# Seven groups of a hybrid encoder block: nine pairs by seven products instead of eight, and four low parts a group made by adding transfers

## The chip, the core and the metric

The kernel runs on one core of one Trainium2 chip. The metric is the device time of one execution in microseconds; lower is better. Five engines matter: PE (TensorE, the matmuls; PEld is its weight load), DVE (VectorE), ACT (ScalarE), POOL (GpSimd) and SP (SyncE, which here only issues DMAs).

## What is computed

One layer of a hybrid streaming encoder, for 256 rows of 4096 float32 values. Cut to what matters:

```python
xn = rms_norm(h, norm_in_g)
proj = xn @ w_in                                  # 4096 x 14336
q, k, v, z_a, a_c, g_c, z_c = split(proj)
y_a = rms_norm(chunked_attention(q, k, v, rel_table), attn_out_g) * silu(z_a)
y_c = rms_norm(conv_module(a_c, g_c, ...), conv_out_g) * silu(z_c)   # one 2048 x 2048 product
h = h + concatenate([y_a, y_c], -1) @ w_out       # 4096 x 4096
gate = sigmoid(rms_norm(h, ple_norm_g) @ w_ple_gate + b_ple_gate)    # 4096 x 4096
h = h + gate * (p @ w_ple)
return rms_norm(h, final_g)
```

Nearly all the work is products of 256 rows with large weights that are read once from HBM.

## The kernel before

**Two parts of every number.** Each operand is split into a high part (a cast to fp32r, which TensorE reads in one pass) and a low part, the float32 value minus the high part, again as fp32r. A product of two blocks is three matmuls: high by high, low by high, high by low (`kind` 0, 1, 2). The weights are split on the fly: SP loads a weight tile `wt` (128 x 2 x 512 values, 512 KB), ScalarE casts it to `wh` (L204), VectorE subtracts to get `wl` (L205). There are five buffers for `wt`, three each for `wh` and `wl`, two each for `uh` and `ul` (below).

**Groups and pairs.** `mixed_product` computes one group: two column blocks of 512 by all 256 rows, accumulated in four PSUM banks over 32 blocks of 128 rows of weights, taken as 16 pairs. A plain pair is 2 blocks x 2 column blocks x 2 halves of the rows x 3 kinds = 24 matmuls. A pair "by sevens" replaces eight block products by seven, in the manner of Strassen and Winograd: P1 to P7, 21 matmuls. For that VectorE forms sums of weight blocks, `ua` (L469, L470) and `ub` (L476, L477), ScalarE and VectorE split them into `uh` and `ul`, and four sums of the left operand (`comb`, kept for each such pair) must have been made before. P1, P5, P6 and P7 collect in four more banks, which VectorE combines after the last pair by sevens (`on_helpers`, `helper_sums`) in two scratch tiles `z` from the pool's tag "stage", which has two buffers.

**The order of the pairs** is written out by hand in texts such as

```python
dense = units("1 0* 3 2* 5 4* 6* 7 8* 9 10* 11 12* 14* 13 15")
```

where a star marks a pair by sevens. A plus marks one whose `ua` is built by a load and a second, adding transfer from GpSimd (L422, L423); the attention and convolution groups use those. Every engine's queue is in order. The program's scheduler decides where instructions of different tiles stand on a queue.

**Stages, in order of time.** Convolution and attention groups of w_in (to about 920 us), two groups of w_pw, the combinations of xT for the coming groups, four groups of gates (`gated`, from about 987 us, order `dense`), four groups of the last projection w_out (the first with order `late`, from about 1316 us, then three with `dense`), four groups of w_ple_gate (to the end). Each gates group ends with products of z and the accumulators on VectorE, the activation Silu on ScalarE, and a last product that is put off (`later`) into the first pairs of the next group. The combinations for pairs by sevens with even numbers are made by `combine_again` and `combined_parts`.

Of the kernel before, what the change touches and what calls it, by code (L numbers as in the profile page):

```python
# [10 lines left out]
F32 = mybir.dt.float32  # L11
F32R = mybir.dt.float32r
# [13 lines left out]
def hybrid_block(  # L26
# [172 lines left out]
    def parts_of(wt, kc, tiles=None):  # L199
# [10 lines left out]
        return (wh, wl), made  # L210

    recent = []

# [46 lines left out]

    def combined_parts(dst, at, s, a, a01, a11, g, then=lambda ins: None):

        a00, a10 = a[:, :P], a[:, P:]
        s3, s5, s2, s4 = (s[:, i * P : (i + 1) * P] for i in range(4))
        stt = nc.vector.scalar_tensor_tensor
        then(nc.vector.tensor_tensor(s3, a00, a10, ALU.subtract))
        then(stt(s5, a11, g, a10, ALU.mult, ALU.subtract))
        then(stt(s2, s5, -1.0, a00, ALU.mult, ALU.subtract))  # L270
        then(stt(s4, a01, g, s2, ALU.mult, ALU.add))

        def split():
            hi, lo = dst[:, at : at + 2, 0, :], dst[:, at : at + 2, 1, :]
            src = s.rearrange("q (i t) -> q i t", t=T)
            then(nc.scalar.copy(hi, src))
            then(nc.vector.tensor_tensor(lo, src, hi.bitcast(F32), ALU.subtract))

        return split
# [6 lines left out]

    def combine_again(dst, at, t, i, rows, then=lambda ins: None):

# [6 lines left out]
        )  # L295
        return combined_parts(dst, at, s, a[:, :T], a[:, T : T + P], a[:, T + P :], 1.0, then)

# [26 lines left out]
    def units(text):  # L324

        return [(int(u.rstrip("*+")), u[-1] if u[-1] in "*+" else "") for u in text.split()]


    dense = units("1 0* 3 2* 5 4* 6* 7 8* 9 10* 11 12* 14* 13 15")
    first = units("0 1 3 5 7 9 11 13 15 2* 8 4* 10 6* 12 14")  # L330
    early = units("1 3 5 0+ 7 9 2+ 11 13 4+ 15 8 6+ 10 12 14")
# [9 lines left out]
    final = units("1 0* 3 2* 5 4* 6* 7 8* 9 10* 12* 11 13 14 15")  # L341
    late = units("1 3 5 7 9 11 13 15 0* 2 4* 6 8* 10* 12 14")

    def mixed_product(
# [13 lines left out]
        n_left = len(left) // 2  # L358
        for n, (_, seven) in enumerate(order[: len(order) - n_left]):
            for name in ("P1", "P5", "P6", "P7", "P2", "P3", "P4") if seven else ("P2", "P3", "P4", "X"):  # L360
                ends[name] = n
# [37 lines left out]
        def add_plain(n, k, wh, wl, **kw):  # L399
            pair = order[n][0]  # L400
            for j in range(2):
                for h in range(NH):
                    name = (("P2", "P3"), ("P4", "X"))[h][j]
                    add(name, block(2 * pair + k, h), (wh[:, j], wl[:, j]), n, k == 1, **kw)

        sums = {}

# [18 lines left out]
        if begin:  # L426
            done, behind = begin(add_plain)
            for ins in behind:
                after.enter_context(tc.issue_after(ins.ins))
        last_seven = max((n for n, (_, seven) in enumerate(order) if seven), default=None)  # L430
        for n, (pair, seven) in enumerate(order):
            if n < done:
# [18 lines left out]
            if not seven:  # L451
                for k in range(2):
                    add_plain(n, k, *parts_of(wts[k], 2)[0])
                fill(fills[n % len(fills)])
                continue
# [15 lines left out]
            with queued_behind(before if seven == "+" else ()):  # L471
                uah, ual = pair_parts(ua)
            w1h, w1l = parts_of(w1, 2)[0]
            if seven == "*" and not sums:
# [5 lines left out]

            def s_of(i):
                t, at = comb[pair] if isinstance(comb, dict) else (comb[pair // 4], pair % 4)
                return [t[:, at + i // 2, q, (i % 2) * P : (i % 2 + 1) * P] for q in range(2)]
# [4 lines left out]
            add("P7", s_of(0), (uah[:, 1], ual[:, 1]), n, True)  # L488
            add("P2", block(k1, 0), (w1h[:, 0], w1l[:, 0]), n, True)
            add("P3", s_of(3), (w1h[:, 1], w1l[:, 1]), n, True)  # L490
            add("P6", s_of(2), (ubh[:, 0], ubl[:, 0]), n, True)
            add("P4", block(k1, 1), (ubh[:, 1], ubl[:, 1]), n, True)
            if begins and on_begin:
                on_begin()
# [564 lines left out]
    for c in range(2, D // NB):  # L1059
        if c % 2 == 0:  # L1060
            comb_tile(xS, 1)
        combine_again(xS[c // 2], 2 * (c % 2), xT[c], 0, sum_rows())()

    def gated(ys, c0, col, r_y, order, ahead):

        _, z = sum_tiles()

        def on_helpers(helper):
            nc.scalar.copy(z[0][0], helper["P1"])
            helper_sums(helper, z)  # L1070
# [33 lines left out]
    for ys, o_z, r_y in ((y_a, o_za, r_a), (y_c, o_zc, r_c)):  # L1104
        for c0 in range(0, len(ys), 2):
            last = ys is y_c and c0 + 2 == len(ys)
            gated(
                ys, c0, o_z, r_y, dense,
                before_last(y_ahead) if last else None,
# [24 lines left out]
    for c0 in range(0, D // NB, 2):  # L1134
# [8 lines left out]
        def on_helpers(helper):  # L1143
# [8 lines left out]
        acc = mixed_product(  # L1152
            w_out[0], c0 * NB, yT, yS, dense if c0 else late, on_helpers,
            ahead=y_ahead if c0 == 0 else before_last(h_ahead) if c0 + 2 == D // NB else None,
            fills=(2,),
        )
        for h, j in QUARTERS:
            hc = hs[c0 + j][:, h, :]
            tt(hc, acc[h][j], hc, ALU.add)
            later.append(partial(square_sum, ssq_h[:, h, c0 + j : c0 + j + 1], hc))  # L1160
    fill(len(later))
    r_h = rstd_of(ssq_h, D, "r_h")
# [8 lines left out]
    def gated_pair(c0, order, ahead):  # L1171

        _, z = sum_tiles()
        rows, fgs = [], []

        def on_begin():
            rows.extend(broadcast_row(b_ple_gate, (c0 + j) * NB, NB) for j in range(2))

        def on_helpers(helper):
            stt(z[0][0], helper["P1"], r_h[:, :1], rows[0], ALU.mult, ALU.add)  # L1180
            helper_sums(helper, z)
# [178 lines left out]
```

## Time and profile before

| | us |
|---|---|
| three runs, median | 2028.87 |
| lowest and highest | 2028.55 and 2030.01 |
| the profiled execution: its span, first to last instruction | 2027.3 |

The median lies 1.6 us above the span of the profiled execution; the part outside the span is what a run needs ahead of the first and behind the last instruction. Of the profile the following views are used: the page (span, chain, costliest groups), the busy time by stretch, the waits, the timeline, and the DMA issues with their time to landing. In a row of groups stand the line, engine, operation, tiles (out<-in), the number of instructions, then busy us and mean ns of one, then idle time ahead of them and what ended it. In a row of waits stand who waited for whom, the us in total, the times, and the longest.

### The profile page before, as it was taken

What the parts mean: (1) busy time and instruction counts of PE and PEld (TensorE: products, weight loads), DVE (VectorE), ACT (ScalarE), POOL (GpSimd) and SP (SyncE); (2) the same over time, 40 slices, a digit from 0 to 9 for tenths busy, and PEclk for the clock granted to TensorE, in tenths of its full rate; (3) what the DMA queues carried; (4) which work ended last, traced back from release to release, by engine and by line L of the source; (5) the groups of instructions that cost most, each with busy time, mean ns of one, the idle gap of its engine ahead of it and who ended that gap; (6) DMA issues with size and microseconds to landing.
All of it is one profiled execution on the core that took longest, in us unless ns stands there. A gap on an engine that the chain in (4) does not pass through costs nothing.

```text
span 2027.3 us, 26222 instructions
## 1 busy us (share of the span) xinstructions
PE 2010.3 (99%) x9064; PEld 1652.2 (81%) x9064; DVE 1917.8 (95%) x2732; ACT 1222.7 (60%) x1591; POOL 46.9 (2%) x50
## 2 busy tenths in 40 slices
PE   9999999999999999999999999999999999999997
PEld 7888888878888888788888888888888888888876
DVE  7999999889999998888899999999999999999998
ACT  7655545665656556776556566676665666665555
POOL 0000000000000000000000000000000000000000
PEclk9999999999999999999999999999999999999999
DMA  8787878678669867556666666676666656666765
GB/s 293 222 237 236 253 219 249 177 227 256 192 198 268 251 202 239 157 176 213 192 210 204 206 203 214 210 239 209 203 210 199 208 191 204 207 219 205 233 206 181
DMA packets 171168, 436.70 MB, mean 215 GB/s; under 512 B 13966, under 2 KB 17182, under 8 KB 171034
## 3 DMA queue, kind: packets, MB, share of 16 engines
q1 hardware_dynamic: 161952, 417.93, 64.1%
q0 software_dynamic: 8432, 16.25, 4.7%
q8 instruction: 71, 1.16, 0.3%
q10 hardware_dynamic: 650, 0.84, 0.1%
q14 instruction: 63, 0.52, 0.1%
HBM read 430.77 MB, written 4.19 MB: 215 GB/s over the span
## 4 chain that ended last, share of the span: by engine, by line
PE 92%; DVE 4%; issue 2%; DMA 1%; ACT 1%; POOLq 0%; POOL 0%; ACTq 0%; DVEq 0%
PE acc L387 71%; PE acc_P L387 17%; DVE wl L205 1%; PE tmp_ps L170 1%; DVE cv L726 1%; PE acc L229 1%; DMA wt<-in_w_in_dram 1%; DVE ul L205 1%; PE tmp_ps L898 0%; PE tmp_ps L882 0%; PE tmp_ps L916 0%; DVE cv L807 0%; PE tmp_ps L921 0%; ACT uh L204 0%; PE acc L375 0%
## 5 line engine op out<-in xcount | busy, mean ns | idle before, releaser
L387 PE MATMUL acc<-wh,big_t 128*128 128x512 f32 x4112 | 1271.6, 391 | 0.9 <-DVE y_c L1051 0.7
L204 ACT CAST wh<-wt 128x1024 fp32r<-128x1024 f32 (+1 forms) x737 | 708.8, 972 | 514.6 <-PE acc L387 359.8
L387 PEld LDWEIGHTS acc<-wh,big_t 128*128 128x128 f32 x4112 | 768.9, 188 | 160.4 <-DVE y_c L1051 1.1
L205 DVE TENSOR_TENSOR wl<-wt,wh 128x1024 fp32r<-128x1024 f32 (+1 forms) x737 | 816.7, 1120 | 33.4 <-ACT wh L204 27.8
L387 PE MATMUL acc<-wl,big_t 128*128 128x512 f32 x2056 | 794.5, 392 | 0.1
L387 PEld LDWEIGHTS acc<-wl,big_t 128*128 128x128 f32 x2056 | 385.5, 188 | 81.6 <-DVE wl L205 2.0
L204 ACT CAST uh<-ua 128x1024 fp32r<-128x1024 f32 x180 | 189.4, 1052 | 95.9 <-DVE ua L470 46.4
L205 DVE TENSOR_TENSOR ul<-ua,uh 128x1024 fp32r<-128x1024 f32 x180 | 219.5, 1220 | 5.0 <-ACT uh L204 3.2
L726 DVE SCALAR_TENSOR_TENSOR cv<-uT,dw,cv 128x255 f32<-128x255 f32 (+23 forms) x480 | 204.2, 465 | 1.1
L387 PE MATMUL acc_P<-uh,big_t 128*128 128x512 f32 x528 | 161.8, 391 | 0.1
L204 ACT CAST uh<-ub 128x1024 fp32r<-128x1024 f32 x92 | 96.8, 1052 | 92.5 <-DVE ub L477 81.1
L205 DVE TENSOR_TENSOR ul<-ub,uh 128x1024 fp32r<-128x1024 f32 x92 | 112.2, 1220 | 6.3 <-ACT uh L204 5.5
L387 PEld LDWEIGHTS acc_P<-uh,big_t 128*128 128x128 f32 x528 | 98.0, 188 | 23.0 <-ACT uh L204 3.5
L387 PE MATMUL acc_P<-ul,big_t 128*128 128x512 f32 x264 | 101.1, 391 | 0.1
L469 DVE TENSOR_TENSOR ua<-wt 128x512 f32<-128x512 f32 x105 | 72.0, 686 | 17.6 <-DMA wt<-in_w_in_dram 11.5
L387 PE MATMUL acc<-uh,big_t 128*128 128x512 f32 x272 | 84.1, 390 | 0.0
L387 PE MATMUL acc_P<-wh,big_t 128*128 128x512 f32 x272 | 84.0, 389 | 0.0
L470 DVE TENSOR_TENSOR ua<-wt 128x512 f32<-128x512 f32 x105 | 71.8, 684 | 3.2 <-DMA wt<-in_w_in_dram 3.1
L387 PE MATMUL acc_P<-uh,comb_t 128*128 128x512 f32 x228 | 70.2, 391 | 0.4 <-ACT uh L204 0.3
L477 DVE TENSOR_TENSOR ub<-ub,wt 128x512 f32<-128x512 f32 x92 | 63.1, 686 | 0.8
L476 DVE TENSOR_TENSOR ub<-ua,wt 128x512 f32<-128x512 f32 x92 | 62.9, 684 | 0.3
L387 PEld LDWEIGHTS acc<-uh,big_t 128*128 128x128 f32 x272 | 51.1, 188 | 10.6
(244 smaller groups left out, 1518.9 us busy)
## 6 DMA issues: line engine op xcount, KB each, us to landing
wt<-in_w_in_dram SPq DMA_DIRECT2D x416, 512.0 KB, 4.6
wt<-in_w_out_dram SPq DMA_DIRECT2D x128, 512.0 KB, 4.2
wt<-in_w_ple_gate_dram SPq DMA_DIRECT2D x128, 512.0 KB, 4.2
wt<-in_w_pw_dram SPq DMA_DIRECT2D x32, 512.0 KB, 4.7
ua<-in_w_in_dram SPq DMA_DIRECT2D x31, 512.0 KB, 4.5
ua<-in_w_in_dram POOLq DMA_DIRECT2D x31, 512.0 KB, 8.4
wt<-in_w_in_dram SPq DMA_DIRECT2D x31, 256.0 KB, 2.9
hc<-in_x_dram SPq DMA_DIRECT2D x8, 512.0 KB, 4.2
```

The source lines that it names most:

```text
L170: nc.tensor.transpose(pt[:, i * T + h * P : i * T + (h + 1) * P], src[:, h, b] if len(src.shape) == 4 else src[:, h, b * P : (b + 1) * P], ...
L204: nc.scalar.copy(wh[:, :kc, :], wt[:, :kc, :]),
L205: nc.vector.tensor_tensor(wl[:, :kc, :], wt[:, :kc, :], wh[:, :kc, :].bitcast(F32), ALU.subtract),
L229: nc.tensor.matmul(acc, a, b[:, k, :], start=kb == 0 and kind == 0, stop=kb == kblocks - 1 and kind == 2,)
L387: nc.tensor.matmul(banks[name], a, b, start=name not in begun, stop=final and ends[name] == n and kind == 2 and not (left and name in "P2 ...
L469: plus(ua[:, 0], w0[:, 0], w0[:, 1])
L470: plus(ua[:, 1], w0[:, 1], w1[:, 1])
L476: plus(ub[:, 0], ua[:, 0], w1[:, 1])
L477: plus(ub[:, 1], ub[:, 0], w1[:, 0])
L726: nc.vector.scalar_tensor_tensor(cv[:, i, PAD - k :], uT[:, i, : T + k - PAD], dw[:, b, k : k + 1], cv[:, i, PAD - k :], ALU.mult, ALU.add,)
```

## The change

In the four groups of gates and the last three groups of w_out the order `dense` gives way to `denser`. Pair 13 is by sevens too, so nine pairs are by sevens and seven plain. Pairs 3, 4, 6 and 10 carry a minus: the low part of their second weight block isn't made by VectorE. ScalarE writes the negated weights, rounded to fp32r and so minus the high part, into a tile `low` of tag "stage" (L217), and GpSimd issues a transfer that loads the same weights from HBM again and adds them to it (L495 for a plain pair, L524 for one by sevens). What then stands in `low` is the low part. The products with it (kind 2: four matmuls for a plain pair, two for one by sevens) are put off until behind the next pair. The combinations for pair 13 have no room of their own: they go into blocks of the operand's tiles that no pair reads any more, since pairs 0, 2, 4 and 6 are by sevens in every one of these groups (`spare_places`, `combine_into_places`), once ahead of the gates and once behind the first group of w_out. The scratch tiles `z` are taken only in `on_helpers`, so that `low` can use their buffers before. All else is as it was: loads, other groups, w_ple_gate with `dense`.

```diff
+    def high_and_minus(wt):
+        wh = wpool.tile([P, KC, NB], F32R, tag="wh", name="wh", bufs=3)
+        nc.scalar.copy(wh, wt)
+        low = spool.tile([P, KC, NB], F32R, tag="stage", name="low")
+        nc.scalar.activation(low, wt, AF.Identity, scale=-1.0)
+        return wh, low
...
     dense = units("1 0* 3 2* 5 4* 6* 7 8* 9 10* 11 12* 14* 13 15")
+    denser = units("1 0* 3- 2* 5 4*- 13* 7 6*- 8* 10*- 9 12* 14* 11 15")
...
+    def spare_places(tiles):
+        return [[t[:, 0, q, P:] for q in range(2)] for t in tiles]
+    def combine_into_places(pair, tiles):
+        rows = sum_rows()
+        places[pair] = spare_places(tiles[:4])
+        t, i = tiles[pair // 2], pair % 2 * 2
+        combine_again(None, None, t, i, rows, at_places=places[pair])()
...
             if not seven:
-                for k in range(2):
-                    add_plain(n, k, *parts_of(wts[k], 2)[0])
+                add_plain(n, 0, *parts_of(wts[0], 2)[0])
+                if by_dma:
+                    wh, low = high_and_minus(wts[1])
+                    nc.gpsimd.dma_start(
+                        low, two_columns(w, 2 * pair + 1, col, apart), accum_op=ALU.add
+                    )
+                    add_plain(n, 1, wh, low, kinds=range(2))
+                    waiting.append((n + 1, partial(add_plain, n, 1, wh, low, kinds=(2,))))
+                else:
+                    add_plain(n, 1, *parts_of(wts[1], 2)[0])
+                add_waiting(n)
...
-            add("P2", block(k1, 0), (w1h[:, 0], w1l[:, 0]), n, True)
-            add("P3", s_of(3), (w1h[:, 1], w1l[:, 1]), n, True)
+            for name, x, j in (("P2", block(k1, 0), 0), ("P3", s_of(3), 1)):
+                part = partial(add, name, x, (w1h[:, j], w1l[:, j]), n, True)
+                part(kinds=range(2 if by_dma else 3))
+                if by_dma:
+                    waiting.append((n + 1, partial(part, kinds=(2,))))
...
+            add_waiting(n)
...
+    combine_into_places(13, xT)
...
-                ys, c0, o_z, r_y, dense,
+                ys, c0, o_z, r_y, denser,
...
-            w_out[0], c0 * NB, yT, yS, dense if c0 else late, on_helpers,
+            w_out[0], c0 * NB, yT, yS, denser if c0 else late, on_helpers,
...
+        if c0 == 0:
+            combine_into_places(13, yT)
```

**PE, second group of gates, pairs 3 and 2.** In the order before, the second block of pair 3 (its weights are `wh_9640` and `wl_9641`), and the beginning of pair 2:

```order
L387 MATMUL acc00_9525<-wh_9640,big_t_228 128x512 x2
L387 MATMUL acc00_9525<-wl_9641,big_t_228 128x512
L387 MATMUL acc10_9527<-wh_9640,big_t_228 128x512 x2
L387 MATMUL acc10_9527<-wl_9641,big_t_228 128x512
L387 MATMUL acc01_9526<-wh_9640,big_t_228 128x512 x2
L387 MATMUL acc01_9526<-wl_9641,big_t_228 128x512
L387 MATMUL acc11_9528<-wh_9640,big_t_228 128x512 x2
L387 MATMUL acc11_9528<-wl_9641,big_t_228 128x512
L387 MATMUL acc_P1_9571<-wh_9660,big_t_228 128x512 x2
```

In the changed kernel the end of pair 2 (weights `9696`, sums `9703`), with what was put off from pair 3 (`low_9670`), and the first row of pair 5:

```order
L420 MATMUL acc01_9554<-wl_9697,comb_t_120 128x512
L420 MATMUL acc_P6_9602<-uh_9703,comb_t_120 128x512 x2
L420 MATMUL acc_P6_9602<-ul_9704,comb_t_120 128x512
L420 MATMUL acc10_9555<-uh_9703,big_t_228 128x512 x2
L420 MATMUL acc10_9555<-ul_9704,big_t_228 128x512
L420 MATMUL acc00_9553<-low_9670,big_t_228 128x512
L420 MATMUL acc10_9555<-low_9670,big_t_228 128x512
L420 MATMUL acc01_9554<-low_9670,big_t_228 128x512
L420 MATMUL acc11_9556<-low_9670,big_t_228 128x512
L420 MATMUL acc00_9553<-wh_9736,big_t_289 128x512 x2
```

The four products with the low part have moved from inside pair 3 to behind pair 2.

**ACT, second group of gates, from the end of pair 0 to pair 5.** Before (`wh_9586` is the second high part of pair 0, `9624` and `9640` are pair 3, `9660` and `9671` pair 2, `9707` and `9723` pair 5):

```order
L204 CAST wh_9586<-wt_9569 128x1024
L204 CAST wh_9624<-wt_9620 128x1024
L204 CAST wh_9640<-wt_9622 128x1024
L204 CAST wh_9660<-wt_9656 128x512
L204 CAST uh_9667<-ua_9664 128x1024
L204 CAST wh_9671<-wt_9658 128x1024
L204 CAST uh_9678<-ub_9675 128x1024
L204 CAST wh_9707<-wt_9703 128x1024
L204 CAST wh_9723<-wt_9705 128x1024
```

Now (`wh_9614` pair 0, `9652` and `9668` pair 3, `9685` and `9696` pair 2, `9736` pair 5; `low_9785` belongs to pair 4, which comes after pair 5):

```order
L204 CAST wh_9614<-wt_9597 128x1024
L217 ACTIVATE low_9670<-wt_9650 128x1024
L204 CAST wh_9652<-wt_9648 128x1024
L215 CAST wh_9668<-wt_9650 128x1024
L204 CAST wh_9685<-wt_9681 128x512
L204 CAST uh_9692<-ua_9689 128x1024
L204 CAST uh_9703<-ub_9700 128x1024
L204 CAST wh_9696<-wt_9683 128x1024
L217 ACTIVATE low_9785<-wt_9770 128x1024
L204 CAST wh_9736<-wt_9732 128x1024
```

Each `low` stands ahead of high parts of blocks that TensorE uses earlier, for pair 4 by a whole pair.

**POOL, from the end of attention to the end of the gates.** Before:

```order
L139 TENSOR_TENSOR r_ln<-r_ln,mhalf 128x2
L139 TENSOR_TENSOR r_a<-r_a,mhalf 128x2
L139 TENSOR_TENSOR r_c<-r_c,mhalf 128x2
L139 TENSOR_TENSOR r_h<-r_h,mhalf 128x2
L1283 TENSOR_TENSOR end<-end,mhalf 128x1 x2
```

Now:

```order
L139 TENSOR_TENSOR r_a<-r_a,mhalf 128x2
L495 DMA low<-in_w_in_dram 128x1024
L139 TENSOR_TENSOR r_c<-r_c,mhalf 128x2
L524 DMA low<-in_w_in_dram 128x1024 x3
L495 DMA low<-in_w_in_dram 128x1024
L524 DMA low<-in_w_in_dram 128x1024 x3
L495 DMA low<-in_w_in_dram 128x1024
```

POOL's queue, empty in these groups before, now holds four transfers a group, one of a plain pair and three of pairs by sevens, and r_c, the scale of the convolution half, has come to stand behind the first of them.

## What was predicted before the run

> **What bounds the kernel now.** I began with the page: the span, the chain that ended last, the costliest group.
>
> ```profile
> span 2027.3 us, 26222 instructions
> ...
> PE 92%; DVE 4%; issue 2%; DMA 1%; ACT 1%; POOLq 0%; POOL 0%; ACTq 0%; DVEq 0%
> ...
> L387 PE MATMUL acc<-wh,big_t 128*128 128x512 f32 x4112 | 1271.6, 391 | 0.9 <-DVE y_c L1051 0.7 <-DVE z L1075 0.2
> ```
>
> TensorE sets the time: 92% of the chain is PE, and its largest group waited 0.9 us in the whole program. A mean of 391 ns is not what one matmul costs, because matmuls overlap. So I went to the timeline of PE alone, inside a gates group.
>
> ```profile
> 1199.64 0.62 PE L387 MATMUL acc<-wh,big_t 128*128 128x512 f32 x2
> ...
> 1203.72 0.62 PE L387 MATMUL acc<-wh,big_t 128*128 128x512 f32 x2
> ```
>
> From 1199.64 to 1203.72 PE starts six threes (two with the high weights, as in these rows, then one with the low): 4.08 us for 18, or 0.227 us each. The trace runs at that step nearly everywhere. The table by stage asks whether other engines are close behind. Its first row is an attention stage that already has adding transfers, the second is one gates group, from the first matmul to the next group's first.
>
> ```profile
> core 0: us, PE busy (x) PEld busy (x) DVE busy (x) ACT busy (x) POOL busy (x), PEclk, DMA share, GB/s
> 200.00:350.00 150.00, 150.00 (x671) 124.25 (x670) 149.86 (x250) 78.75 (x88) 9.74 (x8) 1.00 0.82 238
> ...
> 1068.68:1150.56 81.88, 81.86 (x360) 67.49 (x361) 78.22 (x93) 49.14 (x55) 0.00 (x0) 1.00 0.64 205
> ```
>
> A group is 360 matmuls in 81.9 us, 0.227 us each, at a granted clock of 1.00. VectorE is busy 78.2 of the 81.9, so it has 3.6 us to spare. The waits of two gates groups say who holds whom.
>
> ```profile
> ACT wh L204 <- PE acc L387: 18.3, 21, 1.7
> ...
> DVE ua L469 <- DMA wt<-in_w_in_dram: 3.8, 4, 1.7
> ```
>
> ScalarE waits for PE to give back high-part buffers (21 times), so preparation runs ahead as far as its buffers let it. VectorE waits for loads before its ua, 3.8 us in two groups, and PE does not feel it. PE is the bound, and fewer matmuls mean less time, as long as VectorE and the loads keep up.
>
> **The change part by part.** *Products.* In each of the seven groups a plain pair (24 matmuls) becomes one by sevens (21). That is 7 x 3 = 21 matmuls x 0.227 us = 4.76 us off PE. The delayed third products are moved, not added. This term is the whole gain.
>
> The Trainium skill ("TensorE: Matmul & The Clock Gate", Back-to-back issue gap) gives about 131 ns per matmul for sustained pairs of weight load and matmul with N=512. By that the saving would be an estimated 2.8 us and the time 2026.1. This trace has 227 ns between starts and does not agree with it, so the measurement decides.
>
> *VectorE.* Its instructions overlap too, so I take distances between starts.
>
> ```profile
> 1119.86 1.22 DVE L205 TENSOR_TENSOR wl<-wt,wh 128x1024 fp32r<-128x1024 f32 x1
> 1120.99 0.68 DVE L470 TENSOR_TENSOR ua<-wt 128x512 f32<-128x512 f32 x1
> 1121.59 0.68 DVE L476 TENSOR_TENSOR ub<-ua,wt 128x512 f32<-128x512 f32 x1
> ```
>
> A 128x1024 subtraction takes 1.13 us of the queue, a 128x512 operation 0.60 us. A pair by sevens has five of 0.60 (wl half, two ua, two ub) and three of 1.13: 6.4 us. A plain pair has two of 1.13: 2.3 us. One more by sevens adds 4.1 us, and four low parts that VectorE no longer makes take away 4.5 us. VectorE goes from 78.2 to 77.8 us a group while the group shrinks by 0.68 to 81.2 us, so 3.4 us stay to spare. The new order has three pairs by sevens in a row (6, 8, 10), which the old one never had. Two of those leave a low part out: 5.3 + 6.4 + 5.3 = 17.0 us of VectorE against some 62 matmuls, 14.1 us, 2.9 us behind. The old runs of two (12.8 against 9.5 us) fell 3.3 us behind and PE did not stop, so I put nothing down for it.
>
> *ScalarE.* It writes the negated copy that the transfer adds to.
>
> ```profile
> L204 ACT CAST uh<-ua 128x1024 fp32r<-128x1024 f32 x8 | 8.4, 1056 | 5.8 <-DVE ua L470 5.2 <-PE acc_P L387 0.6
> ...
> L1076 ACT ACTIVATE z<-z,r_x 128x512 f32<-128x512 f32 x5 | 3.4, 718 | 1.7 <-DVE z L1075 1.7
> ```
>
> That operation is not in the trace. It lies between 1.06 us (a cast of the same size) and 1.44 us (twice the 718 ns activation of half the size). I take 1.2, four a group 4.8 us, and the extra pair by sevens adds about 1.7. ScalarE goes from 49 to 56 of 81 us. Behind a "low" that waits for its load stand the high parts of the next block on the same queue. In the order "low" stands about a pair early, where ScalarE was waiting for PE anyway, so I put nothing down. In the gates the first "low" also waits until VectorE has read the last group's z out of the same buffer, which it does during the first two pairs; the transfer's cover, below, starts later by that at most.
>
> *Adding transfers.* The attention stage already runs them (first part), the gates do not (second).
>
> ```profile
> q0 software_dynamic: 2174, 4.19, 16.8%
> ...
> wt<-in_w_in_dram SPq DMA_DIRECT2D x49, 512.0 KB, 5.0
> ...
> ua<-in_w_in_dram POOLq DMA_DIRECT2D x8, 512.0 KB, 8.1
> ```
>
> ```profile
> wt<-in_w_in_dram SPq DMA_DIRECT2D x64, 512.0 KB, 4.2
> ```
>
> One costs 16.8% of 150 us over eight, 3.15 us of all sixteen DMA engines, and lands after 8.1 us. Four more bring a group's DMA share from 0.64 to (52.4 + 12.6) / 81.2 = 0.80. The attention stage ran at 0.82, and PE started 671 matmuls in 150 us, its full step. Does the sum land in time? The low of pair 3 stands on ScalarE's queue before that pair's own high parts, and its product stands behind pair 2. PE has 20 + 21 matmuls to do in between, 9.3 us. For pair 6 it is 19 + 21, 9.1 us, for pairs 4 and 10 some 64, 14.5 us. ScalarE's lead of one and a half pairs of buffers comes on top, so 8.1 us is covered. If it were not, the whole of PE's queue would stand behind the waiting product. POOL has nothing else to do in these groups. Its r_c now stands behind the first transfer, but is wanted two groups later.
>
> *Combinations for pair 13.* Two sets of nine small VectorE operations are new, one before the gates, one after the first group of the last projection.
>
> ```profile
> 950.00:1000.00 50.00, 49.33 (x218) 40.50 (x217) 40.53 (x62) 27.74 (x36) 0.69 (x1) 1.00 0.67 206
> ...
> 1350.00:1400.00 50.00, 50.00 (x225) 41.19 (x225) 48.30 (x69) 30.14 (x37) 0.00 (x0) 1.00 0.69 228
> ```
>
> ```profile
> L291 DVE TENSOR_TENSOR comb<-big_t 128x512 f32<-128x512 f32 x16 | 11.0, 688 | 0.1
> ...
> L268 DVE TENSOR_TENSOR comb<-comb 128x128 f32<-128x128 f32 x31 | 8.9, 287 | 0.9 <-ACT comb L284 0.7
> ```
>
> A set is 0.69 + 8 x 0.29 = 3.0 us. Before the gates VectorE is idle 9.5 of 50 us, which hides it. In the second place it is idle 1.7 of 50, so 0 to 1.3 us can show. I take 0.3, because the two last pairs there are plain and give VectorE time back. The 0.9 us that PE waits at group starts may vanish or double: -0.9 to +0.9, taken as 0.
>
> Sum: -4.76 + 0.3 = -4.5 us. The span goes from 2027.3 to 2022.8. The median of the three runs, 2028.87, lies 1.6 us above the profiled span, and with the same 1.6 the time is 2024.4.
>
> **The rivals.** *Late loads eat part of it.* A load that is issued together with an adding transfer shares the engines with it:
>
> ```profile
> wt<-in_w_in_dram SPq DMA_DIRECT2D x1, 512.0 KB, 8.1
> ua<-in_w_in_dram POOLq DMA_DIRECT2D x1, 512.0 KB, 8.3
> ```
>
> That is 3.9 us later than 4.2, and there are 28 such transfers. The Trainium skill ("DMA: Bandwidth & Descriptors", Issuing engines are not separate DMA queues) says that all issuers' transfers interleave on the same 16 engines. By that rule, the trace agrees: 8.1 beside one, 4.2 without. What an uncovered late load costs stands at 425 to 432 us:
>
> ```profile
> DVE ua L469 <- DMA wt<-in_w_in_dram: 1.1, 1, 1.1
> PE acc_P L387 <- ACT uh L204: 1.0, 1, 1.0
> ```
>
> VectorE waited 1.1 us for a load, PE 1.0. For it: the gates already wait for loads. Against: in 200 to 350 us eight transfers cost PE nothing. At 0.1 to 1.0 us a group the time is 2025.1 to 2031.4, typically 2027.5.
>
> *Slower: the run of 6, 8, 10.* Two of the four transfers fall into the six loads of this run, where VectorE loses ground anyway. If two loads a group come late uncovered, at 1.0 us each, seven groups lose 14 us: 2024.4 + 14 = 2038. It decides from 0.68 us a group, where the gain is gone, and shows as slower by over 0.2% from 1.26 us a group. Against it stands the spare 3.4 us of VectorE.
>
> *More than the matmuls.* If the waits at group starts go as well, it is 2024.4 - 0.9 - 0.3 = 2023.2 or a little less.
>
> **How the numbers follow.** About 0.2%, 4.06 us, is what a measurement of this kernel can tell from no change, so "faster" means under 2024.81. The forecast (2023.4 to 2025.4) gets 0.47, of which 0.39 lies under that line. Late loads get 0.28, slower 0.17, more than the matmuls 0.08. Faster 0.47, same 0.08 + 0.28 = 0.36, slower 0.17. The range from 2023.0 to 2032.0 holds the forecast, the late loads and half of the last case, 0.8 in all. The forecast's own range is 2023.4 to 2025.4.
>
> **What would show it.** Right: seven groups of 357 matmuls in some 81.2 us at 0.227 us each, VectorE still under 78 us in each, no wait of PE for "low", loads of the gates landing at about 5 us. Wrong: PE waiting for uh or wl behind VectorE's ua, above all in pairs 8 and 10; PE waiting for an adding transfer; ScalarE waiting long before "low".

## The result, and the profile after

The changed kernel is slower: 2065.64 us, the median of four runs (2064.26 to 2068.92), against 2029.06 for four runs of the kernel before. The ratio is 1.0183, with a 95% interval of 1.0169 to 1.0198. The profiled execution has a span of 2063.0 us. That is 35.7 more than before, although 21 matmuls (4.76 us) are gone, so 40.5 us were lost somewhere. The page of the changed kernel, with the span, the chain that ended last and two groups; the last row is the first of these groups in the kernel before:

```profile
span 2063.0 us, 26342 instructions
...
PE 81%; DVE 9%; DMA 4%; issue 3%; ACT 2%; ACTq 0%; POOLq 0%; POOL 0%; DVEq 0%; SPq 0%
...
L205 DVE TENSOR_TENSOR wl<-wt,wh 128x1024 fp32r<-128x1024 f32 (+1 forms) x709 | 779.7, 1110 | 59.2 <-ACT wh L204 54.0
...
L420 PE MATMUL acc_P<-ul,big_t 128*128 128x512 f32 x285 | 113.1, 404 | 9.6 <-DVE ul L205 9.5
```

```profile
L205 DVE TENSOR_TENSOR wl<-wt,wh 128x1024 fp32r<-128x1024 f32 (+1 forms) x737 | 816.7, 1120 | 33.4 <-ACT wh L204 27.8
```

PE has fallen from 92% to 81% of the chain; for the most part VectorE and DMA stand in its place. VectorE sat idle 54.0 us ahead of `wl`, waiting for ScalarE's `wh`, against 27.8 before. The gates end 22.0 us later than before (VectorE's last `z<-acc,z` there ends at 1341.7, before at 1319.7 us), the last projection 35.8 us later (its last `hc<-acc,hc` ends at 1692.7, before at 1656.9), and what follows takes as long as before. The granted clock was 0.994 over the span, against 0.998; a kernel below loses as much at 0.998, so the clock isn't the cause. The busy time of 300 us inside the gates says how much work was done there, first in the kernel before, then in the changed one. The count behind PE's busy time is of matmuls.

```profile
1000.00:1300.00 300.00, 299.76 (x1322) 247.61 (x1321) 286.32 (x335) 180.65 (x199) 0.00 (x0) 1.00 0.64 206
```

```profile
1000.00:1300.00 300.00, 284.47 (x1216) 226.58 (x1215) 265.78 (x318) 182.31 (x205) 13.10 (x15) 0.99 0.72 215
```

PE started 106 matmuls fewer, 24.1 us at 0.227. VectorE did not become full, as a VectorE-bound kernel would show: its busy time fell from 286.3 to 265.8. Both engines wait for something else. The waits from 990 to 1310 us name it, first in the kernel before, then in the changed one:

```profile
ACT uh L204 <- DVE ub L477: 37.3, 16, 3.2
ACT wh L204 <- PE acc L387: 35.0, 41, 1.7
...
DVE ua L469 <- DMA wt<-in_w_in_dram: 7.8, 8, 1.7
DVE wl L205 <- ACT wh L204: 3.1, 5, 0.7
...
DVE ua L470 <- DMA wt<-in_w_in_dram: 1.6, 3, 0.9
```

```profile
ACT low L217 <- DMA wt<-in_w_in_dram: 31.8, 12, 4.5
...
DVE wl L205 <- ACT wh L204: 17.2, 15, 4.1
PEld acc_P L420 <- DVE ul L205: 11.9, 12, 1.7
DVE ua L519 <- DMA wt<-in_w_in_dram: 9.7, 11, 3.0
PE acc_P L420 <- DVE ul L205: 7.2, 8, 1.3
```

Read the second from the top: ScalarE stands at `low` until a load lands (12 times; before, it waited for no load), VectorE waits for ScalarE, PE for VectorE. PE never waits for `low` itself. One such case can be followed through the queues. ScalarE:

```profile
1202.03 1.05 ACT L215 CAST wh<-wt 128x1024 fp32r<-128x1024 f32 x1
1207.32 1.06 ACT L217 ACTIVATE low<-wt 128x1024 fp32r<-128x1024 f32 x1 [4.24 <-DMA wt<-in_w_in_dram]
1208.28 1.55 ACT L204 CAST wh<-wt 128x512 fp32r<-128x512 f32 x2
```

SP's issue of the load that this `low` reads, then its time from issue to landing, then the adding transfer issued ahead of it on POOL:

```profile
1198.58 0.33 SPq L482 DMA_DIRECT2D wt<-in_w_in_dram  x1
```

```profile
wt<-in_w_in_dram SPq DMA_DIRECT2D x1, 512.0 KB, 8.7
```

```profile
1196.28 0.86 POOL L524 DMA_DIRECT2D low<-in_w_in_dram  x1 [15.88 <-PE acc L420]
```

VectorE and PE at the same time:

```profile
1204.14 0.69 DVE L532 TENSOR_TENSOR ub<-ub,wt 128x512 f32<-128x512 f32 x1
1208.91 0.69 DVE L205 TENSOR_TENSOR wl<-wt,wh 128x512 fp32r<-128x512 f32 x1 [4.08 <-ACT wh L204]
```

```profile
1207.13 0.39 PE L420 MATMUL acc<-ul,big_t 128*128 128x512 f32 x1
1208.93 0.74 PE L420 MATMUL acc_P<-wh,big_t 128*128 128x512 f32 x2 [1.42 <-ACT wh L204]
```

The `low` is that of pair 10. It stands on ScalarE's queue ahead of the high parts of pair 8, and needs the load of pair 10's second block. That load was issued at 1198.58, 2.3 us behind an adding transfer (another load was issued between the two), and took 8.7 us where the median of before was 4.2. With 4.2 it would have landed at 1202.8, before ScalarE came to `low` at 1203.1, and nobody would have waited for it. So ScalarE stood for 4.24 us, VectorE for 4.08, and PE, whose lead was used up, for 1.42.

The median hides this: in 990 to 1310 us it went only from 4.1 to 4.5 us. But of the loads whose landing the trace gives, 32 of 103 took more than 6 us, and none of 105 before.

### The profile page after: what moved, and what is told of

The parts are those of the page before. It is cut to its first block, busy times and chain, and to the rows that moved or that the text cites. A ratio compares the mean times of both kernels' runs of the same rounds, so it can differ in the third digit from the quotient of the medians.

```text
span 2063.0 us, 26342 instructions
## 1 busy us (share of the span) xinstructions
PE 2024.5 (98%) x9043; PEld 1650.3 (80%) x9043; DVE 1922.4 (93%) x2764; ACT 1255.7 (61%) x1641; POOL 72.4 (4%) x78
## 4 chain that ended last, share of the span: by engine, by line
PE 81%; DVE 9%; DMA 4%; issue 3%; ACT 2%; ACTq 0%; POOLq 0%; POOL 0%; DVEq 0%; SPq 0%
PE acc L420 62%; PE acc_P L420 15%; DVE wl L205 3%; DMA wt<-in_w_out_dram 2%; DVE ul L205 2%; DMA wt<-in_w_in_dram 2%; PE tmp_ps L170 1%; ACT wh L204 1%; DVE cv L787 1%; PE acc L237 1%; DVE ub L531 0%; DVE ua L519 0%; ACT uh L204 0%; DVE ua L518 0%; PE tmp_ps L959 0%
## 5 line engine op out<-in xcount | busy, mean ns | idle before, releaser
L420 PE MATMUL acc<-wh,big_t 128*128 128x512 f32 x4028 | 1241.5, 392 | 3.0 <-DVE z L1138 2.3
L204 ACT CAST wh<-wt 128x1024 fp32r<-128x1024 f32 (+1 forms) x709 | 675.8, 964 | 456.6 <-PE acc L420 336.1
L420 PEld LDWEIGHTS acc<-wh,big_t 128*128 128x128 f32 x4028 | 754.9, 188 | 160.9 <-issue 3.6
L205 DVE TENSOR_TENSOR wl<-wt,wh 128x1024 fp32r<-128x1024 f32 (+1 forms) x709 | 779.7, 1110 | 59.2 <-ACT wh L204 54.0
L420 PE MATMUL acc<-wl,big_t 128*128 128x512 f32 x1944 | 752.6, 393 | 2.8 <-DVE wl L205 2.7
L420 PEld LDWEIGHTS acc<-wl,big_t 128*128 128x128 f32 x1944 | 365.2, 188 | 82.6 <-DVE wl L205 7.4
L420 PE MATMUL acc_P<-uh,big_t 128*128 128x512 f32 x570 | 178.7, 399 | 3.5 <-ACT uh L204 3.4
L205 DVE TENSOR_TENSOR ul<-ub,uh 128x1024 fp32r<-128x1024 f32 x99 | 120.8, 1220 | 2.3 <-PE acc_P L420 0.7
L420 PE MATMUL acc_P<-ul,big_t 128*128 128x512 f32 x285 | 113.1, 404 | 9.6 <-DVE ul L205 9.5
L518 DVE TENSOR_TENSOR ua<-wt 128x512 f32<-128x512 f32 x112 | 76.6, 684 | 16.0 <-DMA wt<-in_w_in_dram 11.0
L519 DVE TENSOR_TENSOR ua<-wt 128x512 f32<-128x512 f32 x112 | 76.6, 684 | 15.0 <-DMA wt<-in_w_in_dram 10.3
L420 PEld LDWEIGHTS acc_P<-ul,big_t 128*128 128x128 f32 x285 | 54.3, 191 | 29.6 <-DVE ul L205 18.5
```

The lines of the kernel that those rows point to most:

```text
L204: nc.scalar.copy(wh[:, :kc, :], wt[:, :kc, :]),
L205: nc.vector.tensor_tensor(wl[:, :kc, :], wt[:, :kc, :], wh[:, :kc, :].bitcast(F32), ALU.subtract),
L420: nc.tensor.matmul(banks[name], a, b, start=name not in begun, stop=final and ends[name] == n and kind == 2 and not (left and name in "P2 ...
L518: plus(ua[:, 0], w0[:, 0], w0[:, 1])
L519: plus(ua[:, 1], w0[:, 1], w1[:, 1])
```

## The experiments

Three explanations were set against each other: the early `low` (ScalarE's queue), the late loads (the transfers share the DMA engines), and VectorE being full. All times are medians, and each ratio is against the kernel before on the same chip.

**Low made late.** `low` is made from the high part, so it can only stand behind it on ScalarE's queue.

```diff
-        nc.scalar.activation(low, wt, AF.Identity, scale=-1.0)
+        nc.scalar.activation(low, wh.bitcast(F32), AF.Identity, scale=-1.0)
```

> The negated copy is made from the high part that ScalarE has just cast, not from the loaded weights, so that it stands behind that cast on ScalarE's queue and waits for no load of its own. All else is as in the changed kernel, the 28 adding transfers too. Theory 1 (ScalarE stands still ahead of the negated copy, 49 us in 21 waits, because it asks for a load some four blocks early, and the high parts behind it come late): these waits vanish, and the time comes down by 30 us or more, to 2024 to 2036 us. Theory 2 (the adding transfers share the DMA engines and make the loads late): the time stays at 2055 us or above. Theory 3 (VectorE can't keep up with nine pairs by sevens, three of them in a row): it stays at 2055 us or above.

2032.94 us, ratio 1.0019 (1.0010 to 1.0029). That one line gives back 33 of the 37 us. The loads are as late as ever, 36 of 105 take more than 6 us, so late loads alone aren't the cause; but the forecast's gain isn't there either. PE waits for the sums now, in 990 to 1310 us:

```profile
PEld acc L420 <- DMA low<-in_w_in_dram: 5.3, 6, 2.2
...
PE acc L420 <- DMA low<-in_w_in_dram: 3.3, 3, 1.7
```

**No adding transfers.** The 28 transfers are left out, so the third products of four blocks a group multiply the negated weights; `low` is early as in the changed kernel.

```diff
-                    nc.gpsimd.dma_start(
-                        low, two_columns(w, 2 * pair + 1, col, apart), accum_op=ALU.add
-                    )
```

(and the same for pairs by sevens)

> The 28 adding transfers are left out, so that the low parts of those blocks are only minus the high parts (that part of the products is not computed); order, negated copies and their place stay as in the changed kernel. Theory 1 (ScalarE's queue is blocked at the negated copy): little changes, 2055 to 2068 us, and ScalarE still waits over 30 us for loads at the negated copies. Theory 2 (shared DMA engines): the time comes down to 2024 to 2036 us. Theory 3 (VectorE's work): 2055 us or above.

2026.6 us, ratio 0.9985 (0.9975 to 0.9994). With the same early `low` on the same queue, ScalarE's wait for loads in 990 to 1310 us has shrunk from 31.8 us to

```profile
ACT low L217 <- DMA wt<-in_w_in_dram: 4.4, 5, 1.3
```

No load of the 105 takes more than 6 us here. So neither explanation is enough alone.

**Both: low late and no transfers**, the fourth corner (the transfers left out as above).

> The changed kernel without its 28 adding transfers and with low made from the high part. It leaves the addition out, so the third products of four blocks a group multiply the negated high part. It is the fourth corner: early low with transfers took 2065.6 us, late low with transfers 2032.9, early low without transfers 2026.6. Theory "both together" (an early low costs only where loads come late): without transfers the place of low is worth 0 to 3 us, so 2023.5 to 2027. Rival "the early low costs by itself": the wait of 9.4 us for loads that was left without transfers also reached PE, and its going brings 4 us or more, 2022.5 or less.

2025.97 us, ratio 0.9980 (0.9971 to 0.9988). The four corners:

| ratio to before | adding transfers | without them |
|---|---|---|
| low early | 1.0183 | 0.9985 |
| low late | 1.0019 | 0.9980 |

Without transfers the place of `low` is worth 0.0005, less than its uncertainty; with them 0.0164, 33 us. With `low` late, the transfers cost 0.0039, 8 us; with it early, 0.0198, 40 us. Most of the loss is the product of the two: late loads, and a queue on which an early reader passes their lateness on.

**Nine pairs by sevens, no minus.** VectorE makes all low parts.

```diff
-    denser = units("1 0* 3- 2* 5 4*- 13* 7 6*- 8* 10*- 9 12* 14* 11 15")
+    denser = units("1 0* 3 2* 5 4* 13* 7 6* 8* 10* 9 12* 14* 11 15")
```

> Nine pairs by sevens in the new order, but every low part is made by VectorE: no negated copies, no adding transfers. VectorE's queue then holds some 82.3 us a group against 81.2 us of matmuls. Theory 1 (blocked ScalarE queue) and theory 2 (shared DMA engines) both take the cause away: VectorE binds with about 1 to 2 us a group, 2030 to 2045 us. Theory 3 (VectorE can't keep up): slower than the changed kernel, 2066 us or above, since VectorE has 4.5 us more to do in each group.

2035.77 us, ratio 1.0029 (1.0018 to 1.0040). This is what a full VectorE looks like, 297.94 of 300 us busy:

```profile
1000.00:1300.00 300.00, 299.52 (x1310) 243.53 (x1309) 297.94 (x356) 185.32 (x207) 0.00 (x0) 1.00 0.66 203
```

Four more low parts a group are 28 x 1.13 = 31.6 us of VectorE; against the corner without transfers they cost 0.0049, 9.9 us. The other 21.7, 3.1 us a group, went into time that VectorE had to spare.

**Eight pairs by sevens, with the minus** on 3, 4, 8 and 10: the transfers without the ninth pair and its places.

```diff
-    denser = units("1 0* 3- 2* 5 4*- 13* 7 6*- 8* 10*- 9 12* 14* 11 15")
+    denser = units("1 0* 3- 2* 5 4*- 6* 7 8*- 9 10*- 11 12* 14* 13 15")
```

> The old order with its eight pairs by sevens, and four low parts a group by negated copy and adding transfer (pairs 3, 4, 8 and 10); no combinations for pair 13. VectorE has 4.5 us less to do a group than before the change. Theory 1 (blocked ScalarE queue) and theory 2 (shared DMA engines): slower than before by 20 to 45 us, 2049 to 2075 us, with ScalarE waiting for loads at the negated copies under theory 1. Theory 3 (VectorE's work and the run of three): as fast as before, 2026 to 2031 us.

2069.14 us, ratio 1.0195 (1.0179 to 1.0210). VectorE has less to do than in the kernel before, and the time is that of the changed kernel, within the uncertainties. With the kernel just above (VectorE full, yet 30 us faster than the changed one) this rules out a full VectorE as the cause.

**Eight with the minus, low late** (both edits).

> The old order with eight pairs by sevens, minus on 3, 4, 8 and 10, and low made from the high part: the transfers without the early low and without more work by sevens. VectorE has 4.5 us less a group than before. Theory "both together": the transfers alone cost little without the early low; 2028 to 2034, with what PE waits for the sums (some 8 us in the kernel with nine) as the upper part. Rival "the transfers themselves": 28 of them slow the loads whatever stands on ScalarE; 2040 or above.

2043.30 us, ratio 1.0071 (1.0056 to 1.0087), where the rival had it. `low` late brings 25 us here too, but 14 us over before stay, which I had not expected: VectorE has 4.5 us a group less to do. VectorE's timeline of this kernel shows a second queue with the same fault:

```profile
1036.79 1.22 DVE L205 TENSOR_TENSOR ul<-ub,uh 128x1024 fp32r<-128x1024 f32 x1
1040.83 0.69 DVE L518 TENSOR_TENSOR ua<-wt 128x512 f32<-128x512 f32 x1 [2.82 <-DMA wt<-in_w_in_dram]
...
1043.98 2.35 DVE L205 TENSOR_TENSOR wl<-wt,wh 128x1024 fp32r<-128x1024 f32 x2
```

The two `wl` of a plain pair, whose high parts ScalarE had already made at 1039.45 to 1041.64, stand behind `ua` of the next pair, which waits for a load.

**The same, with ua behind.** Each `ua` is held behind the last low part of the block ahead of it.

```diff
-                plus(ua[:, 0], w0[:, 0], w0[:, 1])
-                plus(ua[:, 1], w0[:, 1], w1[:, 1])
+                with queued_behind(before if any(m for _, _, m in order) else ()):
+                    plus(ua[:, 0], w0[:, 0], w0[:, 1]), plus(ua[:, 1], w0[:, 1], w1[:, 1])
```

> The kernel with the old order, eight by sevens, minus on 3, 4, 8 and 10 and late low (2043.3 us), with each ua held behind the last low part of the block ahead of it on VectorE's queue. In that kernel VectorE waited 35.0 us for loads in front of ua in 990 to 1310 us, with wl of the plain pair before queued behind. Theory "a late load costs what stands behind its first reader": with wl ahead of ua, PE's wait for wl (2.1 us, and 4.7 of its weight loads) goes, and the time falls to 2030 to 2037. Rival "VectorE needs the loads anyway and the lateness only moves to uh and ul": 2040 to 2046.

2032.71 us, ratio 1.0012 (1.0003 to 1.0021): 12 us back. In 300 us PE now starts 1314 matmuls, and 1283 without the edit:

```profile
1000.00:1300.00 300.00, 299.91 (x1314) 245.40 (x1314) 267.76 (x318) 192.66 (x211) 13.01 (x15) 1.00 0.78 233
```

The kernel before had 1322. The DMA share is higher than in any kernel above, 0.78, and PE hardly waits: in this kernel, where no early reader of a load has others queued behind it, sharing the DMA engines costs little.

**Nine with low late, sums two pairs later.** Back to the changed order; each third product waits one pair longer.

```diff
-                    waiting.append((n + 1, partial(add_plain, n, 1, wh, low, kinds=(2,))))
+                    waiting.append((n + 2, partial(add_plain, n, 1, wh, low, kinds=(2,))))
```

(and the same for pairs by sevens)

> As the kernel that makes low from the high part, but each waiting third product stands behind the second pair after its own instead of the first. Theory "both together": what was left there, some 6 to 8 us over the forecast, was PE waiting for the sums (8.6 us in 990 to 1310 us); with 4.8 us more cover that goes, and the time is 2024 to 2028, with no wait of PE or its weight loads for low above 1 us in all. Rival "the late loads themselves": what was left comes from loads that share the engines with the transfers and reach PE through uh, ul and wl; the waits for low go but others take their place, and the time stays at 2031 or above.

2031.16 us, ratio 1.0009 (1.0000 to 1.0018). PE's waits for `low` are gone, but the time is the rival's: what is left, 0.0029 or 6 us over the corner without transfers, isn't the sums. VectorE waits in front of `ua` in 990 to 1310 us, first this kernel, then that corner:

```profile
DVE ua L518 <- DMA wt<-in_w_in_dram: 6.9, 5, 2.1
DVE ua L519 <- DMA wt<-in_w_in_dram: 5.5, 7, 1.6
```

```profile
DVE ua L516 <- DMA wt<-in_w_in_dram: 1.8, 3, 0.7
DVE ua L515 <- DMA wt<-in_w_in_dram: 0.5, 1, 0.5
```

12.4 us over four groups, 3.1 a group, are as much as VectorE's spare time. In the kernel before it waited 9.4 us at the same places and PE felt nothing, so the sum of these waits isn't yet the loss; but with nine pairs by sevens VectorE has less time left to make them good.

**The same with three transfers**, pair 6 without the minus.

```diff
-    denser = units("1 0* 3- 2* 5 4*- 13* 7 6*- 8* 10*- 9 12* 14* 11 15")
+    denser = units("1 0* 3- 2* 5 4*- 13* 7 6* 8* 10*- 9 12* 14* 11 15")
```

> The kernel with late low and sums two pairs later (2031.2 us) with three transfers a group instead of four: pair 6 keeps its low part on VectorE, which has 78.9 of 81.2 us of work then. Theory "each transfer has its price" (4.6 us for 28, 0.16 us each): seven fewer bring 1.2 us, 2029 to 2030.5. Rival "VectorE is nearer to the bound than to spare": the run 6, 8, 10 then takes 18.1 us of VectorE against 14.1 us of PE, and the time is 2032 to 2036.

2039.01 us, ratio 1.0046 (1.0033 to 1.0058). Fewer transfers are slower, by more than either theory had it: 7 low parts more, 7 x 1.13 = 7.9 us of VectorE, cost 0.0037, 7.5 us. By that, VectorE has next to nothing to spare in this order with the transfers about, while without them it had 3.1 us a group. But all seven low parts stand in the run 6, 8, 10, and what their place costs isn't separated from what their number costs.

**The minus on four plain pairs** (3, 5, 7, 9), so that the run 6, 8, 10 keeps its three low parts.

```diff
-    denser = units("1 0* 3- 2* 5 4*- 13* 7 6*- 8* 10*- 9 12* 14* 11 15")
+    denser = units("1 0* 3- 2* 5- 4* 13* 7- 6* 8* 10* 9- 12* 14* 11 15")
```

> As the kernel with sums two pairs later and low made from the high part, but the minus stands on four plain pairs (3, 5, 7, 9) and on none by sevens; VectorE has the same work a group, but the run 6, 8, 10 keeps its three low parts: 19.2 us of VectorE against 14.1 us of PE instead of 17.0. Theory "the run of three binds VectorE": PE waits for uh or ul in the run and the time is 3 to 8 us above the kernel with minus on sevens. Rival "VectorE's lead covers the run, and only the total counts": within 2 us of it, so 2024 to 2030.

2046.88 us, ratio 1.0087 (1.0073 to 1.0100), 15.7 us more than with the minus on sevens: the direction of the first theory, twice its size. VectorE's work a group is the same, so its total isn't all that counts. It also waits longer in front of `ua` (18.0 us in both rows together, 12.4 there), and PE for `wl` behind it; what of the 15.7 us is the run and what the loads isn't separated.

```profile
DVE ua L518 <- DMA wt<-in_w_in_dram: 13.9, 9, 4.4
...
PE acc L420 <- DVE wl L205: 5.4, 2, 2.8
```

**The run broken up.** At most two pairs by sevens stand in a row; low late, sums two pairs later, four transfers.

```diff
-    denser = units("1 0* 3- 2* 5 4*- 13* 7 6*- 8* 10*- 9 12* 14* 11 15")
+    denser = units("1 0* 3- 2* 5 4*- 13* 7 6*- 8* 9 10*- 12* 11 14* 15")
```

> The kernel with late low and sums two pairs later, with the pairs by sevens in runs of at most two (4 and 13, 6 and 8, 10 and 12) and plain pairs between. Theory "the run of three costs": 2028 to 2030, some 2 us less than with 6, 8, 10 in a row. Rival "the run costs nothing, and only one plain pair is left behind 14 to cover the sums of the helpers": 2031 to 2035.

2030.70 us, ratio 1.0003 (0.9994 to 1.0012), between the two theories. In the gates it runs at PE's full step, 300 / 1320 = 0.227 us a matmul, with the DMA share at 0.78; with the run of three it started 1300.

```profile
1000.00:1300.00 300.00, 299.95 (x1320) 246.78 (x1319) 285.90 (x344) 199.86 (x220) 13.01 (x15) 1.00 0.78 236
```

So in the gates the transfers cost PE next to nothing any more: the last `z<-acc,z` there ends at 1318.4 us, in the corner without transfers at 1317.4. The rest of what is lost against that corner lies in the last projection, whose last `hc<-acc,hc` ends at 1658.0 here and at 1653.3 there. In the kernel with the run of three these ends are 1321.6 and 1659.3: breaking up the run gained 3.2 us in the gates, of which 1.9 were lost again in the projection; why isn't shown. The whole time is within its uncertainty of that kernel's, 1.0009, so the run's price in the whole, 1 us, is not settled.

**Nine with ua behind** (the edit above, in the changed order with low late and sums two pairs later).

> The kernel with nine by sevens, late low and sums two pairs later (2031.2 us), with each ua held behind the last low part of the block ahead of it. Theory "a late load costs what stands behind its first reader": part of the 4.6 us that it lies above the kernel without transfers goes; 2026 to 2030. Rival "the order that the scheduler chose hides VectorE's run of three best": ua comes later, uh and ul with it, and the time is 2031 to 2038.

2034.60 us, ratio 1.0018 (1.0009 to 1.0027). No gain, rather a small loss (the intervals overlap), as its rival had it. VectorE no longer waits for loads, but `ua` comes later, and PE's weight loads wait for `uh` in 990 to 1310 us:

```profile
PEld acc_P L420 <- ACT uh L204: 5.2, 17, 0.7
```

**The same bytes without adding.** The changed kernel (low early), its transfers without `accum_op`; the third products of four blocks multiply the whole weights.

> The changed kernel with low early; its 28 transfers load the same bytes from the same queue but do not add. The third products of four blocks a group then multiply the whole weights. Theory "what the addition costs the DMA engines makes the loads late" (3.15 us of all sixteen engines for an adding transfer, against 1.6 or so for a load by bytes): half the lateness goes, and with it at least half of the 39 us; 2030 to 2046. Rival "any transfer between the loads makes them late": same lateness from the bytes and the queue, 2055 or above.

2038.97 us, ratio 1.0038 (1.0023 to 1.0054): 29 of the 37 us are gone, though the same bytes move at the same places. The transfers' queue in 990 to 1310 us, 16 transfers each, in the changed kernel and in this one (the last column is the share of 16 engines):

```profile
q0 software_dynamic: 2304, 8.39, 15.5%
```

```profile
q0 software_dynamic: 2304, 8.39, 9.5%
...
low<-in_w_in_dram POOLq DMA_DIRECT2D x16, 512.0 KB, 6.1
```

An adding transfer takes 0.155 x 320 / 16 = 3.1 us of all sixteen engines, a plain one 1.9. ScalarE's wait at `low` falls from 31.8 to 15.9 us, and 13 of 105 loads take more than 6 us instead of 32 of 103. So it is for the greater part the adding that makes the loads late. The Trainium skill ("DMA: Bandwidth & Descriptors", Issuing engines are not separate DMA queues) has the transfers of all issuers interleave on the same 16 engines; this agrees, the load followed above took 8.7 us beside an adding transfer, and the median without any was 4.2.

**The copy on GpSimd.** POOL and not ScalarE writes the negated weights.

```diff
-        nc.scalar.activation(low, wt, AF.Identity, scale=-1.0)
+        nc.gpsimd.tensor_scalar(low, wt, -1.0, None, ALU.mult)
```

> The changed kernel, but GpSimd and not ScalarE writes the negated copy; GpSimd then waits for the early load, and has nothing behind that wait but the transfer of the same sum. Theory "both together": ScalarE's high parts no longer stand behind a load, VectorE's wait for wh (17.2 us in 990 to 1310 us) falls under 3 us, and the time is 2024 to 2036, the upper end if GpSimd's copy is so slow that PE waits for the sums. Rival "the late loads themselves": loads land as late as in the changed kernel (a tenth of them after 7.6 us or more), and reach PE without ScalarE's queue; 2050 or above.

2042.59 us, ratio 1.0068 (1.0054 to 1.0082). The wait moved off ScalarE, and VectorE's wait for `wh` fell from 17.2 to 2.1 us, as the first theory has it:

```profile
DVE wl L205 <- ACT wh L204: 2.1, 3, 0.7
```

PE waits for no `low` here either. The time is above its range, and the next kernel bears on why.

**GpSimd subtracts, no transfers.** POOL makes the four low parts a group itself.

```diff
-        nc.scalar.activation(low, wt, AF.Identity, scale=-1.0)
+        nc.gpsimd.tensor_tensor(low, wt, wh.bitcast(F32), ALU.subtract)
```

(the transfers taken out, the third products two pairs later)

> The changed kernel's order, without any adding transfer: GpSimd subtracts the high part from the weights for the four blocks, and their third products stand behind the second pair after. The loads are left alone, and VectorE and ScalarE have no more to do than in the changed kernel. Theory "the transfers were the price": with them gone nine by sevens bring their 4 us, 2024 to 2027, if GpSimd, which took 2.8 to 5.8 us for a negated copy of the same size, makes its four in time. Rival "GpSimd's operation slows VectorE or comes too late": in the kernel with the copy on GpSimd PE's weight loads waited 5.8 us for ul in 990 to 1310 us; 2030 to 2042.

2077.53 us, ratio 1.0235 (1.0221 to 1.0249), the slowest of all and far above both theories, with loads at 4.3 us (median) and no wait of PE for `low`. One of VectorE's groups in 1000 to 1300 us, first here, then in the corner without transfers:

```profile
L516 DVE TENSOR_TENSOR ua<-wt 128x512 f32<-128x512 f32 x31 | 31.9, 1030 | 2.7 <-DMA wt<-in_w_in_dram 2.7
```

```profile
L516 DVE TENSOR_TENSOR ua<-wt 128x512 f32<-128x512 f32 x34 | 23.3, 685 | 1.8 <-DMA wt<-in_w_in_dram 1.8
```

The mean of 1030 ns instead of 685 is made of two kinds. Beside one of GpSimd's subtractions:

```profile
1101.48 2.45 POOL L217 TENSOR_TENSOR low<-wt,wh 128x1024 fp32r<-128x1024 f32 x1 [14.13 <-ACT wh L215]
```

```profile
1101.69 2.78 DVE L525 TENSOR_TENSOR ub<-ua,wt 128x512 f32<-128x512 f32 x1
1104.51 0.69 DVE L526 TENSOR_TENSOR ub<-ub,wt 128x512 f32<-128x512 f32 x1
```

The first `ub` takes 2.78 us and ends half a microsecond behind GpSimd, the second takes the usual 0.69. It is so with all 28: beside each, one VectorE operation took 2.5 to 3.4 us, 60 us more than usual in all, and the time is 0.0255 or 52 us above the corner without transfers. Twenty-seven of them are `ua` or `ub`; the one `wl` shows that subtractions into fp32r aren't spared (1.22 us is usual):

```profile
1440.33 3.43 DVE L205 TENSOR_TENSOR wl<-wt,wh 128x1024 fp32r<-128x1024 f32 x1
```

The Trainium skill ("SBUF — State Buffer", SBUF: two separate sides) says that VectorE operations with two SBUF inputs and GpSimd operations that read SBUF lock a shared pair of ports against each other. The trace agrees: these operations all have two inputs in SBUF. In the kernel with the copy on GpSimd some were longer too, `ul` with a mean of 1289 ns instead of 1220, which bears on its time; how much of it that makes isn't shown.

## Why the prediction was wrong

**The step that failed** is the one on ScalarE: "In the order "low" stands about a pair early, where ScalarE was waiting for PE anyway, so I put nothing down." That is the term of 33 us, with the adding transfers about; without them it is 1 us, less than its uncertainty. ScalarE did have time; but what counted was what stood behind `low` on the queue while it waited for a load four blocks ahead. In the kernel before, ScalarE's longest waits were for VectorE's sums (37.3 us) and for buffers that PE gave back (35.0), and the forecast saw only the second. None was for a load, and VectorE waited just 3.1 us for ScalarE's `wh`; in the changed kernel, with 31.8 us of waits for loads at `low`, that row rose to 17.2. A likely reason, argued and not measured, is that a buffer comes back as PE uses one up, so that a wait for it keeps step with PE, and a wait for a load doesn't.

**The transfers' cover.** That the sum lands after some 8.1 us was near (median 7.3), and PE didn't wait for it. In the changed kernel, 990 to 1310 us:

```profile
DMA to landing us min/median/max: 5.5/7.3/10.0
```

With `low` late, and so the sum too, the cover of 9.1 us no longer held, and PE waited 3.3 us for `low` there. What was left out is the loads: the rival "late loads" had them at 8.1 us (the one followed above took 8.7), but counted one uncovered load at 1.0 us, from a place where VectorE waited 1.1 us for it. Here the wait was up to 4.5 us, on ScalarE, and VectorE and PE waited behind it. "Loads of the gates landing at about 5 us" came true in the median, 4.5 us, and was no sign of being right: the loss came with the third of them that took more than 6. The comparison with the attention stage, whose DMA share of 0.82 cost PE nothing, misled me for the same reason: the share wasn't the trouble (PE ran full at 0.78 with an order that suited it), but what stood early.

**VectorE.** 3.4 us a group to spare was right without transfers (3.1 from two kernels). With the transfers it is gone, in front of `ua` that waits for late loads; this much is argued from the rows, and measured only as the price of seven low parts, 7.5 of 7.9 us, all in one place of the order.

**The matmuls and the places.** The forecast of -4.5 us fits as a sum of what it named: without transfers and with `low` late the kernel, which leaves the addition out, was 0.0020 below before, 4.1 us (2.4 to 5.9). Its two terms weren't measured apart.

**The slower rival** had the sign right and the mechanism wrong. The run 6, 8, 10 was to lose to uncovered loads; but the old order with eight by sevens, which has no such run, lost as much (1.0195). The run may hold 1 us of what remains. Its bounds, 0.68 and 1.26 us a group, were worked out from the 4.76 of the matmuls alone; from the sum of 4.5 they are 0.64 and 1.22.

The forecast itself named, among the signs of being wrong, ScalarE waiting long before `low`. It did, 31.8 us in the gates, and nothing had been put down for it.

No version of the whole computation that I ran is faster than the kernel before; the best, with the run broken up, is level with it. What four adding transfers a group still cost when all is put right, some 4 to 5 us, about equals what the ninth pair brings. Whether a sixth load buffer would free it wasn't tried.

## What to carry to other kernels

When an operation moves to another engine, read on that engine's queue which input it waits for and what is queued behind it; idle time of the engine doesn't tell. A wait that comes from a slow transfer is paid by everything that stands behind its first reader, unless those behind had time to lose, so make an operation that can wait depend on something late, as one changed operand did here for 33 us. And a spare of 4% on an engine is a budget for its waits, not room for more work.

## What the runs showed of the hardware that I had not expected

- Adding costs the DMA engines more than loading: 3.1 us of all sixteen for 512 KB, against 1.9 for the same transfer without adding.
- GpSimd takes 2.4 to 6.4 us for a 128x1024 subtraction (median 2.7), and beside each of the 28 one VectorE operation with two inputs in SBUF took 2.5 to 3.4 us instead of 0.69 or 1.22. Others that ran during the same subtraction kept their usual time.

```profile
L217 POOL TENSOR_TENSOR low<-wt,wh x28: 2425/2734/6437, 993.3 to 1658.1; 128x1024 fp32r<-128x1024 f32 x28
```
